# Attention of an encoder trunk: each link of the softmax chain half a slot later, and the channel-major products copied by ScalarE and split by GpSimd

## The chip, the cores and the metric

The kernel runs on one core of one Trainium2 chip. A core has five engines with instruction streams of their own, which wait for each other through semaphores: PE (TensorE: matrix products and transposes into PSUM), ACT (ScalarE), DVE (VectorE), POOL (GpSimd), and SP (SyncE, which here issues DMA transfers). Each engine works through its stream strictly in order. The metric is the time of one execution in microseconds (us).

## The reference

Two layers on a sequence of 512 frames with 1024 channels, in float32. The even layer mixes frames by causal means (the pooling mixer), the odd one by attention with 16 heads of 64 channels; each is followed by a gated feed-forward part with a short causal convolution. Only the attention matters here:

```python
q = head_rmsnorm(q.reshape(B, S, N_HEADS, HEAD_DIM), q_norm)
k = head_rmsnorm(k.reshape(B, S, N_HEADS, HEAD_DIM), k_norm)
...
s = jnp.einsum('bqhd,bkhd->bhqk', qc, kb).astype(jnp.float32) * scale + bias[None]
valid = (band_chunk + c - LEFT_CHUNKS) >= 0
s = jnp.where(valid[None, None, None, :], s, -1e30)
p = jax.nn.softmax(s, axis=-1).astype(vb.dtype)
return jnp.einsum('bhqk,bkhd->bqhd', p, vb)
...
return o @ w_o
```

A product in which float32 accuracy is wanted is made of several products of a faster matrix type: an operand is split into a rounded part ("hi") and the remainder ("lo"), and hi·hi, hi·lo and lo·hi are added up in PSUM.

## The kernel before

The 512 frames are four row tiles of 128. Before the attention loop the first of four head projections is made, and the values. The loop then runs over 64 softmax tiles in fixed order, `tiles_` (16 heads, four row tiles each); tile `t` of a head has (t+1)·128 keys. One pass `i` of the loop is called an iteration, and it has two half-slots (`place` 2i and 2i+1). The loop is written out inside a manual schedule: every engine's stream has exactly the order in which the code issues its instructions.

A tile goes through the steps of the generator `tile_of`: **scores** (two PE products into a PSUM buffer `sc`, L1046 and L1047), **bias** (one DVE instruction that adds the position bias `B` and finds the minimum, L1051), **exp** (ACT, L1054, which also sums), **recip** (DVE, L1056), **scale** (ACT, L1058), **turn** (PE transposes into a PSUM buffer `tp`, L1062), **hi** (ACT, L1066) and **lo** (DVE, L1068). After the fourth tile of a head `mix` multiplies by the values (PE, L1080, PSUM buffer `oo`); ACT copies one half (`ob`, L1087) and DVE adds (L1091), and for each pair of heads the sum is split into hi (ACT, L1292) and lo (DVE, L1296) by `split_pair`.

Between these steps stand **fillers**, PE products that the loop spreads evenly (`fill`): the three other head projections (`project_heads`, 96 products each, until iterations 3.5, 19.5 and 35.5), then 144 output products (`outputs`, PSUM `wo`, until iteration 72). The weights of a filler come by DMA, and are split by ACT (L102) and POOL (L103), from the twelfth chunk on by POOL alone (L100, L103). A projection's four results are squared on ACT (L1167), summed on DVE (L1174), brought to a reciprocal root by `norm`, `seed` and `better` (DVE L1190 to L1193 last), and scaled by four POOL instructions (L1195), each 128x512.

From each scaled projection `channel_major(p, i)` makes the channel-major operands of the pair of heads `p`: four PE transposes into a PSUM buffer `zt` (L1014), a copy to the rounded `zh` by ACT (L1018), a copy of its upper half by POOL (L1020), and lo parts by DVE, `zl` for i = 0 (L1026) or two half-height `kl` for i = 1 (L1024). Both of these read `zt` in PSUM again. Then SP moves halves between partitions by DMA (L1030). `stages` sets these steps in line, at the iterations with i % 8 in `CM` of the pair before.

`later(engine, fn, n)` puts work into a waiting list, and `extra(engine)` takes from it what has waited n half-slots, one entry at a time, or two when more than one is left. The four PSUM buffers of the tag "S" are shared by `sc`, `zt`, `tp` and `oo`: whoever wants one waits for the last reader of what was in it.

Of the kernel before, what the change touches and what calls it, by code (L numbers as in the profile page):

```python
# [17 lines left out]
F32 = mybir.dt.float32  # L18
F32R = mybir.dt.float32r
AF = mybir.ActivationFunctionType  # L20
OP = mybir.AluOpType
# [3 lines left out]
S = 512  # L25
D = 1024
# [17 lines left out]
BANKS = {"PQ": 2, "SS": 4}  # L44


LAG, LAGM = 2, 2
FE = (3.5, 19.5, 35.5)
FO = LAG + 6
CM = (2, 3)  # L50


KIND = "uuppp" + "s" * 17
# [19 lines left out]
def trunk(ctx: ExitStack, tc: tile.TileContext, xt, xT, cols, band, edge, poolw, gv, wout, wqk, wv, wo, rel, out):  # L73
    nc = tc.nc
# [14 lines left out]
    def psum(tag, name, bufs=2):  # L89
        return ps.tile([P, S], F32, name=name, tag=tag, bufs=bufs)  # L90
# [3 lines left out]
    def g_tile(name):  # L94
        return tmp.tile([P, S], F32, name=name, tag="g", bufs=6)
# [31 lines left out]
    def run(steps):  # L127
        step = None
        for step in steps:
            pass  # L130
        return step
# [231 lines left out]
    gq = consts.tile([P, 2], F32, name="gq")  # L363
# [553 lines left out]
    def attention():  # L917
# [7 lines left out]
        KL = [[big.tile([P, S], F32R, name=f"kl{b}{e}") for e in range(2)] for b in range(2)]  # L925
# [70 lines left out]
        def last_output(after):  # L996

            for d in range(KD):
                hi, lo = w[18 + d // 4]
                o = psum("PQ"[d % 2], f"wo{d}_6")  # L1000
                for p in (6, 7):
                    s = slice((d % 4 * 2 + p - 6) * P, (d % 4 * 2 + p - 5) * P)
                    yield from mm3(o, hi[:, s], lo[:, s], XS[p], XS[KD + p], p == 6, p == 7)
                nc.vector.tensor_add(X[d], o, X[d])
                after(d)
                if d == 1:
                    parts(19)

        def channel_major(p, i):

            zt = psum("S", f"zt{p}_{i}", 4)
            for t in range(TT):
                j = 4 * i + 2 * (p % 2)
                nc.tensor.transpose(zt[:, t * P:(t + 1) * P], Z[p // 2, t][:, j:j + 2, :].rearrange("p h d -> p (h d)"), ident)  # L1014
            zh, z2 = (big.tile([P, S], F32R, name=f"z{c}{p}_{i}", tag="zqk", bufs=8) for c in "h2")
            zl = None if i else g_tile(f"zl{p}_{i}")
            yield
            nc.scalar.activation(zh, zt, AF.Copy, scale=gq[:, i:i + 1])  # L1018
            yield
            nc.gpsimd.tensor_copy(z2[HD:], zh[HD:].bitcast(F32))  # L1020
            if i:
                for e in range(2):
                    hs = slice(e * HD, (e + 1) * HD)
                    nc.vector.scalar_tensor_tensor(KL[p % 2][e][hs], zt[hs], gq[hs, i:i + 1], zh[hs].bitcast(F32), op0=OP.mult, op1=OP.subtract)  # L1024
            else:
                nc.vector.scalar_tensor_tensor(zl, zt, gq[:, i:i + 1], zh.bitcast(F32), op0=OP.mult, op1=OP.subtract)  # L1026
            yield
            moves = [(z2[:HD], (z2 if i else zl)[HD:]), (zh[HD:], (zh if i else zl)[:HD])]
            for o, x in moves:
                nc.sync.dma_start(o.bitcast(F32), x if x.dtype == F32 else x.bitcast(F32))  # L1030
            QK[p, i] = (zh, z2)
# [39 lines left out]
        def mix(h):  # L1071

            p, e = divmod(h, 2)
            hs = slice(e * HD, (e + 1) * HD)
            oo = psum("S", f"oo{h}", 4)
            if p not in O2:
                O2[p] = big.tile([P, S], F32, name=f"o2_{p}", tag="o2", bufs=4)
            for c in range(2):
                for j in range(TT):
                    nc.tensor.matmul(oo[:, j * P:], V[j, h // 4][:, h % 4].rearrange("p a d -> p (a d)"),  # L1080
                                     PT[e][c][:, 4 * j:3 * j + TT].rearrange("p t q -> p (t q)"),
                                     start=j == 0 and c == 0, stop=j == TT - 1 and c == 1)
            ob = g_tile(f"ob{h}")
            other = slice(HD - e * HD, 2 * HD - e * HD)

            def copy():
                nc.scalar.activation(ob[hs], oo[other], AF.Copy)  # L1087
                later("D", add)

            def add():  # L1090
                nc.vector.tensor_add(O2[p][hs], oo[hs], ob[hs])  # L1091
                if e:
                    mixed.add(p)

            later("A", copy)

# [6 lines left out]
        for i in range(2):  # L1103
            run(channel_major(0, i))
# [11 lines left out]
        def parts(k):  # L1116

            w[k] = [wp.tile([P, 1024], F32R, name=f"hw{k}_{c}", tag=f"w{c}", bufs=2) for c in "hl"]
            split(raws[k], *w[k], None if k == 19 else nc.gpsimd, nc.gpsimd if 12 <= k < 19 else None)
# [6 lines left out]
        tiles_ = [(h, t) for h in range(H) for t in range(TT)]  # L1126
        nb = len(tiles_)
        place = 0
        waiting = {"A": [], "D": []}
        mixed, kept, moved, scaled = set(), set(), set(), set()  # L1130

        def later(engine, fn, n=1):
            waiting[engine].append((place + n, fn))

        def extra(engine, all_=False):

            n = 0
            q = waiting[engine]
            while q and q[0][0] <= place and (n == 0 or all_ or len(q) > 1 and n < 2):
                q.pop(0)[1]()  # L1140
                n += 1

# [118 lines left out]
        copied, used = set(), []  # L1261
        fillers = [(project_heads(1), 96, -3, FE[0]), (project_heads(2), 96, FE[0], FE[1]), (project_heads(3), 96, FE[1], FE[2]), (outputs(), 144, FE[2], nb + FO)]
        cur, done = 0, 0

        def fill(upto):

            nonlocal cur, done
            while cur < len(fillers):
                g, n, a, b = fillers[cur]
                due = n * (upto - a) / (b - a)  # L1270
                while done < min(due, n):
                    next(g)
                    done += 1
                if upto < b:
                    return
                run(g)
                cur, done = cur + 1, 0
# [3 lines left out]
        def step(j, name):  # L1281

            if 0 <= j < nb:
                if j not in gens:
                    assert all((tiles_[j][0] // 2, i) in QK for i in range(2))
                    gens[j] = tile_of(*tiles_[j])
                assert next(gens[j]) == name

        def split_pair(p):

            def hi():
                nc.scalar.activation(XS[p], O2[p], AF.Copy)  # L1292
                later("D", lo)

            def lo():
                nc.vector.tensor_sub(XS[KD + p], O2[p], XS[p].bitcast(F32))  # L1296
                kept.add(p)

            later("A", hi)

        def stages(p, i):

            g = channel_major(p, i)
            assert p // 2 == 0 or p // 2 in scaled
            next(g)

            def scale():
                next(g)
                later("D", low)

            def low():
                next(g)
                later("D", lambda: run(g), 2)

            later("A", scale)

        order = {mybir.EngineType.PE, mybir.EngineType.DVE, mybir.EngineType.Activation, mybir.EngineType.Pool, mybir.EngineType.SP}
        with tc.manual_schedule(engines=order):
            split_asked = 0
            fill(0)  # L1320
            for i in range(nb + LAG + LAGM):
                place = 2 * i
                step(i, "scores")
                if i % 4 == 2 and i // 4 + 1 < H:
                    biases(i // 4 + 1)
                step(i - 1, "recip")
                step(i - 3, "hi")
                step(i - 1, "scale")
                extra("A")
                extra("D")  # L1330
                step(i, "bias")
                fill(i + 0.45)
                if i % 8 in CM and i // 8 + 1 < NPAIR:
                    stages(i // 8 + 1, CM.index(i % 8))
                place = 2 * i + 1
                step(i, "exp")
                step(i - LAG, "turn")
                step(i - 3, "lo")
                extra("D")
                extra("A")  # L1340
                fill(i + 0.9)
                j2 = i - LAG - LAGM
                if 0 <= j2 < nb and j2 % TT == TT - 1:
                    mix(tiles_[j2][0])
                fill(i + 1)
                while split_asked in mixed and len(used) > 8 + split_asked // 2:
                    split_pair(split_asked)
                    split_asked += 1
            while waiting["A"] or waiting["D"] or cur < len(fillers):
                place += 1  # L1350
                extra("A", True)
                extra("D", True)
                while split_asked in mixed:
                    split_pair(split_asked)
                    split_asked += 1
                fill(min(place / 2 + 0.5, nb + FO))
        assert len(kept) == NPAIR
        return last_output
# [92 lines left out]
```

## Time and profile before

| | |
|---|---|
| time, three runs | 979.63, 979.70, 979.99 us; median 979.7 us |
| profiled execution | 980.12 us, of which the span of the trace is 978.3 us |
| granted TensorE clock | 1.00 throughout |
| scores of the first and of the last tile start | 452.37 and 606.29 us |

Times in the profile count from the start of the span. A row of the profile is a group of instructions: the source line, the engine and operation, what it writes and reads, the form, how many (x), their busy time and the mean of one, and the idle time of the engine just before them with what ended it. A PE row of 128x512 lasts 0.39 us, but such products follow each other every 0.23 us: they overlap in the pipeline. "PEld" is the loading of weights, ahead of the product.

### The profile page before, as it was taken

The page shows a single profiled execution, that of the slowest core. Times are in us where ns is not written, and L with a number is a line of the kernel's source. Part 1 is how long each engine was busy: PE and PEld are TensorE (multiplying, and loading weights), DVE is VectorE, ACT ScalarE, POOL GpSimd, SP SyncE. Part 2 cuts the span into 40 slices and gives each one's busy share as a digit, 9 for nine tenths or more (in the row PEclk, how much of TensorE's full clock was granted, in tenths as well). Part 3 has the DMA queues.
Part 4 walks back from the last instruction along what each step waited for, and adds up shares of the span by engine and source line. Part 5 has one row for each costly group of instructions (what it writes and reads, how often), then busy time and mean ns, then how long its engine had stood idle before and what let it go on. Part 6 is the DMA issues. An engine that isn't in the chain of part 4 may idle for free.

```text
span 978.3 us, 13709 instructions
## 1 busy us (share of the span) xinstructions
PE 963.7 (98%) x4982; PEld 815.6 (83%) x4982; DVE 811.7 (83%) x1461; ACT 576.5 (59%) x989; POOL 105.7 (11%) x92
## 2 busy tenths in 40 slices
PE   9999999999999999999999999999999999999998
PEld 8788988888888888888887778788988888888886
DVE  8999999999899754443777777899989999989953
ACT  7665564664555443345887888646555565556531
POOL 2300000000000013214434433100000000000000
PEclk9999999999999999999999999999999999999999
DMA  8222332332333234233343333323232342322323
GB/s 340 80 88 74 110 114 73 119 119 92 103 94 107 83 90 139 87 108 97 103 119 86 95 74 119 100 75 111 93 113 77 101 131 88 123 94 84 109 82 111
DMA packets 37427, 102.82 MB, mean 105 GB/s; under 512 B 4432, under 2 KB 7904, under 8 KB 37360
## 3 DMA queue, kind: packets, MB, share of 16 engines
q1 hardware_dynamic: 37296, 101.90, 32.8%
q8 instruction: 39, 0.64, 0.3%
q14 instruction: 28, 0.23, 0.1%
q0 software_dynamic: 32, 0.04, 0.0%
q10 hardware_dynamic: 32, 0.00, 0.0%
HBM read 95.60 MB, written 2.14 MB: 100 GB/s over the span
## 4 chain that ended last, share of the span: by engine, by line
PE 86%; DVE 6%; ACT 4%; issue 2%; DMA 1%; SPq 0%; DVEq 0%; ACTq 0%
PE st_m L610 11%; PE out L124 8%; PE out L123 8%; PE out L125 8%; PE st_m L612 6%; PE st_t L610 6%; PE gv L124 4%; PE gv L125 4%; PE gv L123 4%; PE st_t L612 3%; PE st_b L610 3%; PE qk L123 2%; PE qk L125 2%; PE qk L124 2%; PE v L124 1%
## 5 line engine op out<-in xcount | busy, mean ns | idle before, releaser
L124 PE MATMUL out<-one,ow_h 128*128 128x512 f32 x224 | 88.0, 393 | 0.0
L123 PE MATMUL out<-one,ow_h 128*128 128x512 f32 x224 | 87.9, 392 | 0.0
L125 PE MATMUL out<-one,ow_l 128*128 128x512 f32 x224 | 87.8, 392 | 0.0
L833 DVE TENSOR_TENSOR X<-out,X 128x512 f32<-128x512 f32 (+1 forms) x65 | 44.5, 685 | 48.9 <-PE out L125 48.6
L409 ACT ACTIVATE ow_h<-wo_r 128x640 fp32r<-128x640 f32 (+1 forms) x64 | 50.4, 788 | 56.2 <-PE out L124 46.3
L610 PE MATMUL st_m<-two,g_h 128*128 128x512 f32 x240 | 75.0, 394 | 0.0
L610 PE MATMUL st_m<-h,g_h 128*128 128x512 f32 x240 | 74.0, 390 | 0.0
L410 DVE TENSOR_TENSOR ow_l<-wo_r,ow_h 128x640 fp32r<-128x640 f32 (+1 forms) x64 | 57.1, 892 | 2.6 <-ACT ow_h L409 2.6
L424 DVE SCALAR_TENSOR_TENSOR c<-a,col,c 128x511 f32<-128x511 f32 (+1 forms) x76 | 57.0, 753 | 0.0
L610 PEld LDWEIGHTS st_m<-h,g_h 128*128 128x128 f32 x240 | 45.1, 188 | 10.2
L612 PEld LDWEIGHTS st_m<-two,g_l 128*128 128x128 f32 x240 | 45.1, 188 | 9.4
L610 PEld LDWEIGHTS st_m<-two,g_h 128*128 128x128 f32 x240 | 44.1, 188 | 10.0 <-ACT w L619 0.8
L103 POOL TENSOR_TENSOR hw_l<-hw_r,hw_h 128x1024 fp32r<-128x1024 f32 x19 | 45.9, 2417 | 51.9 <-ACT hw_h L102 51.3
L619 ACT ACTIVATE w<-st_m 128x512 f32<-128x512 f32 x30 | 18.0, 599 | 56.4 <-PE st_m L612 56.4
L1054 ACT ACTIVATE sb<-sb,mx 128x128 f32<-128x128 f32 (+1 forms) x64 | 35.9, 560 | 23.9 <-DVE mx L1051 23.5
L612 PE MATMUL st_m<-h,g_l 128*128 128x256 f32 x240 | 48.3, 283 | 0.0
L1051 DVE CUSTOM_DVE_ANT_0 sb<-sc,B 128x128 f32<-128x128 f32 (+1 forms) x64 | 31.0, 485 | 20.3 <-PE sc L1047 19.7
L125 PEld LDWEIGHTS out<-one,ow_l 128*128 128x128 f32 x224 | 42.3, 189 | 6.3
L612 PE MATMUL st_m<-two,g_l 128*128 128x256 f32 x240 | 47.6, 280 | 0.0
L124 PEld LDWEIGHTS out<-one,ow_h 128*128 128x128 f32 x224 | 42.4, 189 | 6.2 <-DVE one L435 0.3
L123 PEld LDWEIGHTS out<-one,ow_h 128*128 128x128 f32 x224 | 42.4, 189 | 6.1
L421 ACT ACTIVATE c<-a,col 128x512 f32<-128x512 f32 x38 | 30.7, 814 | 25.1 <-DVE a L768 23.5
(396 smaller groups left out, 2980.8 us busy)
## 6 DMA issues: line engine op xcount, KB each, us to landing
gv_r<-gv SPq DMA_DIRECT2D x86, 512.0 KB, 3.8
wo_r<-wout SPq DMA_DIRECT2D x32, 384.0 KB, 3.1
wo_r<-wout SPq DMA_DIRECT2D x32, 320.0 KB, 2.9
hw_r<-wqk SPq DMA_DIRECT2D x12, 512.0 KB, 4.0
wv_r<-wv SPq DMA_DIRECT2D x8, 512.0 KB, 3.4
hw_r<-wo SPq DMA_DIRECT2D x8, 512.0 KB, 4.5
xt<-xt SPq DMA_DIRECT2D x4, 512.0 KB, 5.2
X<-xT SPq DMA_DIRECT2D x8, 256.0 KB, 7.6
```

Of the source, the lines that this page charges most:

```text
L103: return (eng or nc.vector).tensor_sub(lo, raw, hi.bitcast(F32))
L123: yield nc.tensor.matmul(o, sh, mh, start=first, stop=False, **how)
L124: yield nc.tensor.matmul(o, sh, ml, start=False, stop=False, **how)
L125: yield nc.tensor.matmul(o, sl, mh, start=False, stop=last, **how)
L409: nc.scalar.activation(hi[:, :n], raw[:, :n], AF.Copy)
L410: return hi, lo, lambda: nc.vector.tensor_sub(lo[:, :n], raw[:, :n], hi[:, :n].bitcast(F32))
L424: nc.vector.scalar_tensor_tensor(c[:, j:], a[:, :S - j], cw[2 - j], c[:, j:], op0=OP.mult, op1=OP.add)
L610: nc.tensor.matmul(o, hi[:, c], B[i, name], start=first and i == 0, stop=False, **how)
L612: nc.tensor.matmul(o[:, 0], lo[:, c], B[i, name][:, 0], start=False, stop=i == 3, **how)
L833: nc.vector.tensor_add(X[d][:, fs], o[:, fs], X[d][:, fs])
L1051: nc.vector.tensor_tensor_reduce(out=s_, in0=sc[:, :n], in1=BT[h % 2][:, :n][:, ::-1], scale=1.0, scalar=3e38, op0=OP.add, op1=OP.min, acc ...
L1054: nc.scalar.activation(s_, s_, AF.Exp, scale=-1.0, bias=mx[:, 0:1], accum_out=mx[:, 1:2])
```

## The change

Each link of a tile's chain is issued half a slot later: exp of tile i-1 now stands in the first half of iteration i (before: exp of tile i in its second half), recip of tile i-1 in the second half, scale of tile i-2 in the second half, turn of tile i-3 (before: i-2), hi and lo of tile i-4 (before: i-3), and `mix` one iteration later. The channel-major work starts one iteration earlier (`CM` (1, 2) for (2, 3)). In it ACT first copies `zt`, scaled, to a float32 tile `zf` in SBUF, and from that makes `zh`; the lo parts are made by POOL from `zf` and `zh`, so that PSUM is read once. The DMA moves wait in a list of their own, "S". `extra` takes a second entry by another rule. The output fillers run a little slower within the loop and faster behind it.

```diff
-LAG, LAGM = 2, 2
+LAG, LAGM = 3, 2
-CM = (2, 3)
+CM = (1, 2)
...
-            nc.scalar.activation(zh, zt, AF.Copy, scale=gq[:, i:i + 1])
+            zs = g_tile(f"zf{p}_{i}")
+            nc.scalar.activation(zs, zt, AF.Copy, scale=gq[:, i:i + 1])
+            yield
+            nc.scalar.activation(zh, zs, AF.Copy)
...
-                    nc.vector.scalar_tensor_tensor(KL[p % 2][e][hs], zt[hs], gq[hs, i:i + 1], zh[hs].bitcast(F32), op0=OP.mult, op1=OP.subtract)
+                    nc.gpsimd.tensor_sub(KL[p % 2][e][hs], zs[hs], zh[hs].bitcast(F32))
...
-                nc.vector.scalar_tensor_tensor(zl, zt, gq[:, i:i + 1], zh.bitcast(F32), op0=OP.mult, op1=OP.subtract)
+                nc.gpsimd.tensor_sub(zl, zs, zh.bitcast(F32))
...
-            while q and q[0][0] <= place and (n == 0 or all_ or len(q) > 1 and n < 2):
+            while q and q[0][0] <= place and (n == 0 or all_ or n < 2 and (place < 16 or len(q) > (1 if engine == "D" else 3))):
...
+                if cur == 3:
+                    due = 104 * (upto - a) / (nb - a) if upto < nb else 104 + 5.6 * (upto - nb) if upto < nb + 5 else 132 + 3 * (upto - nb - 5)
...
-                later("D", low)
-
-            def low():
-                next(g)
-                later("D", lambda: run(g), 2)
+                later("A", high)
+
+            def high():
+                next(g)
+                next(g)
+                later("S", lambda: run(g), 5 if i else 4)
...
-                step(i - 1, "recip")
-                step(i - 3, "hi")
-                step(i - 1, "scale")
+                extra("S")
+                step(i - LAG - 1, "hi")
+                step(i - 1, "exp")
                 extra("A")
                 extra("D")
                 step(i, "bias")
...
-                step(i, "exp")
+                extra("S")
+                step(i - 2, "scale")
+                extra("A")
                 step(i - LAG, "turn")
-                step(i - 3, "lo")
+                step(i - LAG - 1, "lo")
+                step(i - 1, "recip")
                 extra("D")
-                extra("A")
```

Besides, the last split of weights (`parts(19)`) stands one output group earlier, and `split_pair` is also asked for right behind the DVE addition that completes a pair.

Where this moves instructions is seen in the streams. First ACT around the channel-major work of pair 3 (iterations 18 and 19 before, 17 and 18 after); `sb` are softmax tiles with L1054 or L1057 the exponent and L1058 or L1061 the scaling, `pt` the hi parts. Before:

```order
L1018 ACTIVATE zh_0_4814<-zt_0_4809,gq 128x512
L1066 ACTIVATE pt0h<-tp_0_4818 128x128
L1058 ACTIVATE sb_2_4803<-sb_2_4803,mx_2_4804 128x384
L1167 ACTIVATE zs_1_4833<-z_1_4821 128x512
L1054 ACTIVATE sb_3_4837,mx_3_4838<-sb_3_4837,mx_3_4838 128x512
L1159 ACTIVATE z_2_4856<-qk_2_4400 128x512
L1018 ACTIVATE zh_1_4848<-zt_1_4843,gq 128x512
```

The same place in the changed kernel:

```order
L1019 ACTIVATE zf_0_4828<-zt_0_4779,gq 128x512
L1069 ACTIVATE pt1h<-tp_3_4830 128x4x128
L1057 ACTIVATE sb_2_4814,mx_2_4815<-sb_2_4814,mx_2_4815 128x384
L1171 ACTIVATE zs_1_4846<-z_1_4812 128x512
L1061 ACTIVATE sb_1_4773<-sb_1_4773,mx_1_4774 128x256
L1019 ACTIVATE zf_1_4855<-zt_1_4820,gq 128x512
L1069 ACTIVATE pt0h<-tp_0_4857 128x128
L1057 ACTIVATE sb_3_4848,mx_3_4849<-sb_3_4848,mx_3_4849 128x512
L1021 ACTIVATE zh_0_4784<-zf_0_4828 128x512
```

Before, scaling of tile 2 came directly ahead of the exponent of tile 3; now scaling of tile 1 stands between the exponents of tiles 2 and 3, and each channel-major product has two ACT copies, the second (`zh`) some eight rows behind the first (`zf`).

Second, POOL around the scaling of the last projection (`z_2`, `z_3`, the last two of four) and the channel-major work of pair 6. Before:

```order
L1195 TENSOR_TENSOR z_2_5364<-z_2_5364,qk_y 128x512
L1195 TENSOR_TENSOR z_3_5407<-z_3_5407,qk_y 128x512
L1020 CAST z_0_5570<-zh_0_5569 64x512
L100 CAST hw_h<-hw_r 128x1024
L103 TENSOR_TENSOR hw_l<-hw_r,hw_h 128x1024
L1020 CAST z_1_5602<-zh_1_5601 64x512
```

After:

```order
L1199 TENSOR_TENSOR z_2_5400<-z_2_5400,qk_y 128x512
L1199 TENSOR_TENSOR z_3_5391<-z_3_5391,qk_y 128x512
L1023 CAST z_0_5555<-zh_0_5554 64x512
L1029 TENSOR_TENSOR zl_0_5556<-zf_0_5558,zh_0_5554 128x512
L1023 CAST z_1_5594<-zh_1_5593 64x512
L1027 TENSOR_TENSOR kl_3629<-zf_1_5596,zh_1_5593 64x512
L1027 TENSOR_TENSOR kl_3630<-zf_1_5596,zh_1_5593 64x512
```

Three subtractions for each pair have come into POOL's stream, between the scaling and the splitting of weights.

Third, PE at the transposes of pair 6, which read the four scaled tiles. Before, they stood in iteration 42, behind the scores of tile 2 of head 10:

```order
L1046 MATMUL sc_2_5550<-zh_1_5356,zh_0_5322 128x384
L1047 MATMUL sc_2_5550<-kl_3631,zh_0_5322 128x384
L125 MATMUL wo_0_5545<-two_96,hw_l 128x512
L123 MATMUL wo_0_5545<-two_96,hw_h 128x512
L1014 MATMUL zt_0_5564<-ident,z_0_5278 128x128
L1014 MATMUL zt_0_5564<-ident,z_1_5329 128x128
L1014 MATMUL zt_0_5564<-ident,z_2_5364 128x128
L1014 MATMUL zt_0_5564<-ident,z_3_5407 128x128
```

After, they stand in iteration 41, behind the scores of tile 1:

```order
L1049 MATMUL sc_1_5539<-zh_1_5341,zh_0_5300 128x256
L1050 MATMUL sc_1_5539<-kl_3631,zh_0_5300 128x256
L123 MATMUL wo_0_5397<-two_97,hw_h 128x512
L1014 MATMUL zt_0_5549<-ident,z_0_5287 128x128
L1014 MATMUL zt_0_5549<-ident,z_1_5328 128x128
L1014 MATMUL zt_0_5549<-ident,z_2_5400 128x128
L1014 MATMUL zt_0_5549<-ident,z_3_5391 128x128
L1065 MATMUL tp_2_5560<-ident,sb_2_5460 128x128 x3
```

They have moved up by one iteration, and the transposes of a softmax tile (`tp`) follow them at once.

More of the change, by code (lines that the diff above doesn't have):

```diff
@@ L1004, in last_output @@
                 nc.vector.tensor_add(X[d], o, X[d])
+                if d == 0:
+                    parts(19)
                 after(d)
-                if d == 1:
-                    parts(19)
         def channel_major(p, i):
@@ L1093, in add @@
                     mixed.add(p)
+                    split_pairs()
             later("A", copy)
@@ L1128, in attention @@
         place = 0
-        waiting = {"A": [], "D": []}
+        waiting = {"A": [], "D": [], "S": []}
         mixed, kept, moved, scaled = set(), set(), set(), set()
@@ L1299, in split_pair, with split_pairs @@
             later("A", hi)
+        split_asked = 0
+        def split_pairs():
+            nonlocal split_asked
+            while split_asked in mixed and len(used) > 8 + split_asked // 2:
+                split_pair(split_asked)
+                split_asked += 1
         def stages(p, i):
@@ L1318, in attention @@
         with tc.manual_schedule(engines=order):
-            split_asked = 0
             fill(0)
@@ L1345, in attention @@
                 fill(i + 1)
-                while split_asked in mixed and len(used) > 8 + split_asked // 2:
-                    split_pair(split_asked)
-                    split_asked += 1
+                split_pairs()
             while waiting["A"] or waiting["D"] or cur < len(fillers):
                 place += 1
+                assert not waiting["S"]
                 extra("A", True)
                 extra("D", True)
-                while split_asked in mixed:
-                    split_pair(split_asked)
-                    split_asked += 1
                 fill(min(place / 2 + 0.5, nb + FO))
```

## The prediction

> **What bounds the kernel now.** I begin with the engines' shares on the page, and the chain that ended last.
>
> ```profile
> PE 963.7 (98%) x4982; PEld 815.6 (83%) x4982; DVE 811.7 (83%) x1461; ACT 576.5 (59%) x989; POOL 105.7 (11%) x92
> PE 86%; DVE 6%; ACT 4%; issue 2%; DMA 1%; SPq 0%; DVEq 0%; ACTq 0%
> ```
>
> PE is busy 98% of the span, and the change neither adds nor removes a PE product. It can win only time in which PE waits, within the loop that it touches. So the second view is busy time by stretches. I cut the loop at the starts of the scores of every eighth tile, so that each row is one pair of heads (the last one is what follows the loop).
>
> ```profile
> core 0: us, PE busy (x) PEld busy (x) DVE busy (x) ACT busy (x) POOL busy (x), PEclk, DMA share, GB/s
> 452.37:476.88 24.51, 24.21 (x124) 20.26 (x123) 13.58 (x44) 18.21 (x43) 8.92 (x6) 1.00 0.33 89
> 476.88:496.26 19.38, 19.38 (x109) 16.49 (x109) 12.01 (x37) 16.05 (x39) 9.54 (x8) 1.00 0.46 135
> 496.26:516.81 20.55, 19.69 (x110) 16.42 (x109) 16.36 (x48) 17.40 (x43) 6.62 (x5) 1.00 0.35 97
> 516.81:539.20 22.39, 20.28 (x108) 16.39 (x109) 16.32 (x42) 18.71 (x45) 11.29 (x10) 1.00 0.37 93
> 539.20:558.61 19.41, 18.02 (x101) 14.59 (x100) 16.28 (x49) 16.58 (x43) 6.86 (x6) 1.00 0.38 107
> 558.61:577.11 18.50, 16.68 (x93) 13.23 (x94) 14.16 (x44) 15.66 (x40) 9.95 (x10) 1.00 0.33 83
> 577.11:594.40 17.29, 16.04 (x93) 13.10 (x91) 14.07 (x41) 14.07 (x36) 6.60 (x5) 1.00 0.32 92
> 594.40:609.29 14.89, 14.89 (x87) 12.61 (x87) 12.18 (x39) 12.95 (x36) 3.45 (x2) 1.00 0.41 123
> 609.29:630.00 20.71, 20.19 (x93) 16.17 (x93) 17.18 (x27) 14.49 (x23) 3.44 (x2) 1.00 0.39 118
> ```
>
> PE's idle time is length less busy: 0.30, 0, 0.86, 2.11, 1.39, 1.82, 1.25, 0 and 0.52 us, together **8.25 us**. A stop costs more than that, because a product's row lasts longer than the distance to the next one:
>
> ```profile
> 525.72 0.40 PE L123 MATMUL qk<-hw_h,two 128*128 128x512 f32 x1
> 525.96 0.39 PE L124 MATMUL qk<-hw_l,two 128*128 128x512 f32 x1
> ```
>
> Rows of 0.40 us start 0.24 us apart, so the first 0.16 us of a stop still count as busy. The second to fourth stretches hold the same products (109, 110 and 108 records), and the second has no stop: against its 19.38 us the next two are 1.17 and 3.01 us longer, for 0.86 and 2.11 us of idle rows. That is a factor of 4.18/2.97 = 1.41, and all stops cost about 8.25 × 1.41 = **11.6 us**. More than this the change cannot win. The view of waits, PE alone from 445 to 640 us, says on what:
>
> ```profile
> PE tp L1062 <- DVE kl L1024: 3.5, 5, 0.8
> PE sc L1046 <- DVE mx L1051: 2.6, 3, 1.3
> PE tp L1062 <- DVE zl L1026: 0.7, 2, 0.5
> PE sc L1046 <- DMA zh<-zh: 0.3, 1, 0.3
> PE wo L125 <- DVE hw_l L103: 0.2, 1, 0.2
> ```
>
> The first and third are one thing: transposes of a softmax tile wait for a PSUM buffer that the lo parts of the channel-major work still read, 4.2 us of rows, so 5.9 us. Scores that wait for the bias instruction of an earlier tile: 2.6, so 3.7 us. The rest is 8.25 - 6.8 = 1.45, so 2.0 us.
>
> **What is removed.** The lo parts no longer read PSUM:
>
> ```profile
> L1024 DVE SCALAR_TENSOR_TENSOR kl<-zt,gq,zh 64x512 fp32r<-64x512 f32 x14 | 10.5, 749 | 3.5 <-ACT zh L1018 3.4
> L1026 DVE SCALAR_TENSOR_TENSOR zl<-zt,gq,zh 128x512 f32<-128x512 f32 x7 | 5.3, 751 | 3.1 <-ACT zh L1018 2.9
> L1018 ACT ACTIVATE zh<-zt,gq 128x512 fp32r<-128x512 f32 x14 | 9.4, 673 | 0.3 <-PE zt L1014 0.3
> ```
>
> Before, a `zt` buffer came free after 0.67 us of ACT, an idle gap ahead of the first (3.4 us before `kl` and 2.9 before `zl`, in all), and one or two DVE rows of 0.75 us; now it is free after the one ACT copy (of the same form as L1018, so 0.67 us). The 5.9 us go whole; what is late next is that ACT copy, priced below. DVE is relieved of 14 × 0.75 + 7 × 0.75 = 15.8 us. It was busy 115 us of the 157 us of the first eight stretches and is then near 99. With this, and with a whole iteration between the exponent and its reciprocal, the bias instructions come earlier. They were late where DVE had work in front of them; the worst such place is a score 1.34 us late, behind a DVE instruction that ran long:
>
> ```profile
> 525.15 0.50 PE L1046 MATMUL sc<-zh,zh 128*128 128x512 f32 x1 [1.34 <-DVE mx L1051]
> 522.58 1.98 DVE L1296 TENSOR_TENSOR two<-o,two 128x512 fp32r<-128x512 f32 x1
> 521.63 2.38 POOL L103 TENSOR_TENSOR hw_l<-hw_r,hw_h 128x1024 fp32r<-128x1024 f32 x1 [1.36 <-ACT hw_h L102]
> L1296 DVE TENSOR_TENSOR two<-o,two 128x512 fp32r<-128x512 f32 x8 | 8.2, 1029 | 0.4 <-ACT two L1292 0.2
> ```
>
> Eight of these have a mean of 1.03 us, and one took 1.98 us while POOL worked. Such meetings stay, and POOL will be busier; so I count 2.7 of the 3.7 us as gone, with bounds of 1.0 and 3.7. The Trainium skill, "SBUF — State Buffer", section "Who interferes with whom", says that a DVE instruction with two SBUF inputs contends with a GpSimd instruction that reads SBUF, and that the later one blocks; the 1.98 us agree with that. By that page alone each of the eight could meet one of POOL's new subtractions, and the term would fall to its lower end, the sum to 976.0 us. Of the remaining 2.0 us I count 0.9 as gone (0 to 1.5): the wait for `hw_l` goes with the earlier `parts(19)`, the DMA wait may stay. Removed: 5.9 + 2.7 + 0.9 = **9.5 us**.
>
> The view of waits has larger rows than these, and they are no gain:
>
> ```profile
> ACT sb L1054 <- DVE mx L1051: 23.5, 33, 4.2
> DVE mx L1056 <- ACT sb L1054: 14.3, 34, 0.8
> ```
>
> ACT and DVE wait for each other in the chain of a tile, 38 us. The change takes most of that away, since now exp follows its bias by a half-slot and recip its exp by another. But neither engine is the bound, and where PE runs without a stop (the second stretch) they wait as well.
>
> **What is added: a later scaling for earlier transposes.** The first transposes of pairs 4 and 6 read a projection that POOL scales only after `better`. They move up one iteration (41 for 42, 25 for 26).
>
> ```profile
> L1195 POOL TENSOR_TENSOR z<-z,qk_y 128x512 f32<-128x512 f32 x12 | 12.1, 1044 | 10.5 <-DVE qk_y L1193 7.6 <-DVE mx L1056 2.8
> 516.22 4.05 POOL L1195 TENSOR_TENSOR z<-z,qk_y 128x512 f32<-128x512 f32 x4 [2.93 <-DVE qk_y L1193]
> 558.03 4.05 POOL L1195 TENSOR_TENSOR z<-z,qk_y 128x512 f32<-128x512 f32 x4 [4.72 <-DVE qk_y L1193]
> 562.85 0.63 PE L1014 MATMUL zt<-ident,z 128*128 128x128 f32 x4
> 560.45 0.40 PE L124 MATMUL wo<-two,hw_h 128*128 128x512 f32 x1
> 519.11 0.40 PE L123 MATMUL qk<-hw_h,two 128*128 128x512 f32 x1
> 557.87 0.69 DVE L1051 CUSTOM_DVE_ANT_0 sb<-sc,B 128x512 f32<-128x512 f32 x1
> ```
>
> For pair 6 the scaling ended at 558.03 + 4.05 = 562.08, and the transposes came at 562.85. In the new place they stand behind one output product, the one at 560.45, so they would be wanted at 560.7, and the last of the four 0.3 us later, at 561.0 (the four have a row of 0.63 us): 1.1 us before the last scaled tile. `better` now stands behind the bias of tile 39 (the 0.69 us at 557.87) instead of ahead of it, but that bias began only 0.7 us ahead of the scores of tile 40 (558.61), in iterations of some 2.4 us; DVE ran late there and will be less late. I let the start lie between 1.1 us earlier and 1.0 later, which gives a wait of 0 to 2.1 us, and take 1.4. For pair 4 the scaling ended at 520.27, and the transposes are wanted behind the three products that begin at 519.11, at 519.8, the last at 520.1: 0 to 1.2, I take 0.6. Together **2.0 us** (0 to 3.3).
>
> **ACT.** It gets 14 more copies of 128x512 from SBUF within the loop:
>
> ```profile
> L1167 ACT ACTIVATE zs<-z 128x512 f32<-128x512 f32 x12 | 7.5, 623 | 0.0
> ```
>
> Two in each stretch but the last, 1.2 us. PE's needs without stops are 19.4 us in the fourth stretch, 19.41 - 1.39 × 1.41 = 17.4 in the fifth, 15.9 in the sixth and 15.5 in the seventh. ACT then needs 19.9, 17.8, 16.9 and 15.3: 0.5, 0.4 and 1.0 us more than PE in three of them. Its rows overlap by about 0.1 us back to back, so this shortage of 1.9 us is an upper end; I take **1.2 us** (0 to 1.9).
>
> **A buffer within one iteration.** At the first transposes of each pair after the first, `zt` has taken one more buffer, and the following `tp` needs the one that the bias of the same iteration frees. PE's cover is one to three products of 0.23 us and four short transposes. If DVE is held by one reciprocal or lo part, it is late by a few tenths: seven times 0.13, **0.9 us** (0 to 1.8).
>
> **POOL.** The 21 subtractions have the form of L1195, 1.04 us (bounds for a half-height one: 0.61 us by the row below, 1.04 us), 21.8 us in the loop.
>
> ```profile
> L1020 POOL CAST z<-zh 64x512 fp32r<-64x512 f32 x14 | 8.5, 611 | 31.3 <-ACT zh L1018 22.3 <-issue 8.0 <-POOL hw_l L103 0.8
> L103 POOL TENSOR_TENSOR hw_l<-hw_r,hw_h 128x1024 fp32r<-128x1024 f32 x16 | 38.7, 2420 | 31.2 <-ACT hw_h L102 30.6
> z<-z SPq DMA_DIRECT2D x8, 128.0 KB, 2.2
> ```
>
> POOL's 63 us of the first eight stretches become 85 of about 150, so its own work is covered. An operand is needed by the scores two iterations (4 us) after its lo part; the move takes 2.2 us to land, so I cost this at nothing, and up to 1.5 us if POOL's queue is late. The Trainium skill, "GPSIMD Engine Reference", section "4.1 Engine selection", advises against elementwise work with two inputs on this engine, as about 2 times slower than VectorE. The rows say 1.04 against 0.75 us, 1.4 times. With a factor of 2 the subtractions would take 21 × 1.5 = 31.5 us and POOL 95 of 150 us, which would still be covered, but would bring the third rival below closer.
>
> **The sum.** 9.5 - 2.0 - 1.2 - 0.9 = 5.4 us. Against the profiled execution, 980.12 us, that is 974.7; the median of the runs lies 0.4 us below it, so **974.3 us**.
>
> **Rivals.**
> (a) *All waits added are hidden.* After one stop each later engine has caught up, so the three added terms overlap: only the 2.1 us of old waits stay, a gain of 9.5 us, **970.2 us**. For it speaks that DVE loses 14% of its work; against it that POOL's scaling is a chain that nothing shortens.
> (b) *ACT takes the place.* The second copy and the shortage fall into the same stretches as the scaling; ACT's lag of up to 1.9 us is then met again by every following wait of scores and transposes, 4 us more than I count. The gain is 1.4 us: **978.3 us**. ACT at 18.7 of 22.4 us in the fourth stretch speaks for it.
> (c) *Slower: POOL's queue in order.* Ahead of the last scaling POOL now has two subtractions for pair 5 and the splitting of a weight chunk by itself, 1.04 + 2.42 us. If these begin just before `better` ends, scaling starts 3.5 us later, pair 4 loses 2.1 us by its two subtractions in the same way, and the next weight chunk comes late for the output products, 2 to 3 us: 8 us against a gain of 5.4, **982.3 us**. It decides once scaling starts over about 3 us behind `better` at both places. Against it: POOL waited 4.72 and 2.93 us ahead of them.
> (d) *The chain was no cause.* The freed buffers only move PE's wait on to the bias or to the turning of the next tile, since PE meets the same chain a moment later: no change, **979.7 us**. Against it stands the second stretch, where the same chain has no stop.
>
> **How the numbers follow.** Chances: forecast 0.52 (972 to 976.5), (a) 0.20, (b) 0.14, (c) 0.08, (d) 0.06. A measurement of this kernel tells about 0.2%, 2 us, from no change, so faster means below 977.7: the forecast, (a) and a little of (b), 0.75. Slower is (c), 0.08; the rest, 0.17, is the same. For 8 in 10 the range leaves out (c), half of (d) and the far end of (a): 969.5 to 979.7 us.
>
> **What would show it.** In the changed profile the waits of `tp` on `kl` and `zl` are gone, and DVE's time in the first eight stretches is near 99 us. `zt` waits for POOL at two places, about 1.4 and 0.6 us. PE's idle in the nine stretches is near 4.4 us (6.2 us by 1.41) instead of 8.25. Were waits on POOL over 4 us, (c) is right; many waits of `tp` or `sc` on ACT mean (b). Idle time as before with other names at its side would make the prediction wrong, and so would a stop outside the loop.

## The result: slower, and the profile after

| | before | after |
|---|---|---|
| median | 979.74 us (6 runs, 979.63 to 982.19) | 983.59 us (6 runs, 982.22 to 985.79) |
| ratio | | 1.0036, 95% interval 1.0020 to 1.0052 |
| profiled execution, span | 980.12, 978.3 us | 982.51, 980.7 us |
| mean granted clock | 1.0 | 0.994 to 0.998, in every run |

The change makes the kernel 0.36% slower. The forecast was 974.3 us, range 969.5 to 979.7. The first view is again busy time by stretches of the profiled execution, cut at the starts of the scores of every eighth tile; the columns are as before (PE, PEld, DVE, ACT, POOL, then clock and DMA).

```profile
452.30:474.96 22.66, 22.66 (x114) 18.82 (x113) 11.38 (x36) 16.43 (x39) 12.50 (x9) 1.00 0.37 115
474.96:494.28 19.32, 19.32 (x109) 16.50 (x108) 9.84 (x38) 17.07 (x43) 13.66 (x11) 1.00 0.39 108
494.28:516.31 22.03, 19.75 (x110) 16.37 (x108) 14.16 (x45) 20.29 (x51) 9.91 (x7) 1.00 0.26 75
516.31:537.08 20.77, 19.84 (x108) 16.59 (x109) 12.46 (x40) 17.50 (x42) 15.39 (x12) 1.00 0.42 121
537.08:556.74 19.66, 17.43 (x99) 14.46 (x98) 12.71 (x40) 17.57 (x46) 10.13 (x9) 1.00 0.29 79
556.74:575.33 18.59, 17.11 (x90) 14.28 (x91) 12.62 (x43) 15.09 (x40) 14.15 (x12) 0.91 0.37 84
575.33:593.52 18.19, 15.82 (x90) 12.66 (x89) 13.91 (x43) 16.27 (x44) 10.77 (x10) 1.00 0.28 76
593.52:609.79 16.27, 16.10 (x90) 13.67 (x91) 11.00 (x39) 12.27 (x34) 5.02 (x3) 1.00 0.46 141
609.79:630.00 20.21, 20.21 (x99) 16.78 (x98) 15.93 (x26) 12.13 (x20) 3.44 (x2) 1.00 0.36 115
```

Length less busy time gives PE idle of 0, 0, 2.28, 0.93, 2.23, 1.48, 2.37, 0.17 and 0 us: 9.5 us, where before it was 8.25. DVE has lost what it was to lose (98 us in the first eight stretches, from 115), POOL has 92 for 63. And in one stretch the clock is 0.91. The view of waits shows PE's idle time under quite different names, and the same view of SP's queue (DMA issues) what the last of them comes from.

```profile
PE sc L1049 <- DMA zh<-zh: 3.1, 2, 1.7
PE sc L1049 <- DVE qk_t L1194: 2.3, 1, 2.3
PE wo L124 <- DVE two L1302: 1.5, 1, 1.5
PE zt L1014 <- POOL z L1199: 0.9, 2, 0.7
PE wo L123 <- DVE z L1161: 0.9, 1, 0.9
PE tp L1065 <- DVE mx L1054: 0.5, 1, 0.5
...
SPq L1033 <- POOL kl L1027: 14.8, 8, 2.2
```

The many waits of `tp` on `kl` and `zl` are gone, and those of scores on the bias but for 0.2 us. In their place stand a few long ones. Three of them are the first scores of heads 6, 10 and 14, at the heads of the odd pairs 3, 5 and 7. One is put down to `qk_t` on DVE, which the scores do not read; the timelines of POOL, SP and PE there (start, length, engine, what) show that a DMA lands just ahead of it, as for the other two:

```profile
508.05 2.41 POOL L103 TENSOR_TENSOR hw_l<-hw_r,hw_h 128x1024 fp32r<-128x1024 f32 x1
510.52 0.61 POOL L1023 CAST z<-zh 64x512 fp32r<-64x512 f32 x1
511.21 2.71 POOL L1027 TENSOR_TENSOR kl<-zf,zh 64x512 fp32r<-64x512 f32 x2
...
511.16 0.46 SPq L1033 DMA_DIRECT2D z<-z  x1
513.95 0.46 SPq L1033 DMA_DIRECT2D zh<-zh  x1
...
516.31 0.36 PE L1049 MATMUL sc<-zh,zh 128*128 128x256 f32 x1 [2.28 <-DVE qk_t L1194]
```

The second move, `zh<-zh`, writes the lower half of `zh` over its upper half, and POOL's second subtraction still has to read that upper half. POOL ends at 513.92, SP issues the move at 513.95, such a move lands 2.2 us later (the median), and the scores begin at 516.31; PE's last product before them ended at 514.03. Before the change DVE read that half straight after ACT had written it, and the move was issued 8.5 us ahead of the same scores (516.81):

```profile
506.68 1.51 DVE L1024 SCALAR_TENSOR_TENSOR kl<-zt,gq,zh 64x512 fp32r<-64x512 f32 x2 [0.90 <-ACT zh L1018]
508.26 0.46 SPq L1030 DMA_DIRECT2D zh<-zh  x1
```

The other two are put down to the move itself (1.3 and 1.7 us).

### The profile page after: what moved, and what is told of

It reads as the page before. It is cut to its first block, busy times and chain, and to the rows that moved or that the text cites. A ratio compares the mean times of both kernels' runs of the same rounds, so it can differ in the third digit from the quotient of the medians.

```text
span 980.7 us, 13735 instructions
## 1 busy us (share of the span) xinstructions
PE 964.4 (98%) x4982; PEld 817.4 (83%) x4982; DVE 793.9 (81%) x1437; ACT 580.1 (59%) x1005; POOL 137.4 (14%) x116
## 4 chain that ended last, share of the span: by engine, by line
PE 89%; DVE 6%; ACT 3%; issue 1%; DMA 1%; POOL 0%; DVEq 0%; SPq 0%; ACTq 0%; POOLq 0%
PE st_m L610 11%; PE out L124 8%; PE out L125 8%; PE out L123 8%; PE st_m L612 6%; PE st_t L610 6%; PE gv L124 3%; PE gv L125 3%; PE gv L123 3%; PE st_t L612 3%; PE st_b L610 3%; PE qk L125 3%; PE qk L123 3%; PE qk L124 3%; PE oo L1083 2%; PE v L124 1%
## 5 line engine op out<-in xcount | busy, mean ns | idle before, releaser
L1054 DVE CUSTOM_DVE_ANT_0 sb<-sc,B 128x128 f32<-128x128 f32 (+1 forms) x64 | 31.2, 487 | 59.8 <-PE sc L1050 57.1
L148 POOL TENSOR_TENSOR n_acc<-n_acc,n_sq 128x512 f32<-128x512 f32 x7 | 9.6, 1368 | 328.1 <-ACT n_sq L146 328.1
```

The source lines that it names most:

```text
L1054: nc.vector.tensor_tensor_reduce(out=s_, in0=sc[:, :n], in1=BT[h % 2][:, :n][:, ::-1], scale=1.0, scalar=3e38, op0=OP.add, op1=OP.min, acc ...
```

## The experiments

Each kernel was timed in several rounds beside the kernel before on the same chip. The edits are shown against the changed kernel unless said otherwise. The interval of the changed kernel itself is 1.6 us to either side, so smaller differences to it show little by themselves.

| kernel | median, us | ratio to before | 95% interval |
|---|---|---|---|
| e1_swap | 982.48 | 1.0024 | 1.0013 to 1.0036 |
| e2_order_alone | 976.54 | 0.9965 | 0.9953 to 0.9977 |
| e3_split_alone | 991.52 | 1.0118 | 1.0104 to 1.0133 |
| e4_odd_early | 981.65 | 1.0009 | 1.0001 to 1.0018 |
| e5_even_late | 973.62 | 0.9932 | 0.9918 to 0.9945 |
| e6_copies_dve | 987.53 | 1.0073 | 1.0060 to 1.0085 |
| e7_zf_dve | 980.48 | 0.9999 | 0.9991 to 1.0008 |
| e8_copy_first | 972.47 | 0.9920 | 0.9906 to 0.9933 |
| e9_no_overwrite | 982.47 | 1.0022 | 1.0013 to 1.0031 |
| e10_all_early | 978.87 | 0.9987 | 0.9978 to 0.9995 |
| e11_best | 974.25 | 0.9939 | 0.9927 to 0.9952 |
| e12_two_turns | 978.78 | 0.9984 | 0.9975 to 0.9993 |
| e13_no_overwrite_zf_dve | 977.39 | 0.9974 | 0.9965 to 0.9982 |
| e14_no_overwrite_two_turns | 976.86 | 0.9968 | 0.9955 to 0.9980 |
| e15_split_best | 977.86 | 0.9974 | 0.9965 to 0.9983 |

### The two halves of the change

**e2_order_alone** keeps the new order and puts the old channel-major work back, with the moves where the changed kernel has them:

```diff
-            zs = g_tile(f"zf{p}_{i}")
-            nc.scalar.activation(zs, zt, AF.Copy, scale=gq[:, i:i + 1])
-            yield
-            nc.scalar.activation(zh, zs, AF.Copy)
+            nc.scalar.activation(zh, zt, AF.Copy, scale=gq[:, i:i + 1])
...
-                    nc.gpsimd.tensor_sub(KL[p % 2][e][hs], zs[hs], zh[hs].bitcast(F32))
+                    nc.vector.scalar_tensor_tensor(KL[p % 2][e][hs], zt[hs], gq[hs, i:i + 1], zh[hs].bitcast(F32), op0=OP.mult, op1=OP.subtract)
```

> The new order with the old channel-major work: ScalarE makes zh straight from PSUM, VectorE the lo parts from PSUM. Theory A: the waits of the first scores on the moves go (6 us), but waits of tp on kl and zl come back in part; 975 to 979 us. Rival B (ScalarE's load): also faster, 976 to 980 us, but with ScalarE's busy time 8 us lower in the loop being what changed. Rival C (the order itself makes the loss): 982 us or more.

**e3_split_alone** is the reverse: the old order, with `channel_major` as the change has it.

> The old order with the new channel-major work (copy to zf, zh from zf by ScalarE, subtractions by POOL). Theory A: the work begins one iteration later than in the changed kernel, so the moves land later still, at every pair: waits of scores on moves above 6 us, 984 to 990 us, while waits of tp on lo parts are gone. Rival C (order): no slower than before, 976 to 980 us.

Measured: 976.5 us, and 991.5 us, which is above what was expected of e3. So the order gains 0.35%, and the new channel-major work costs 7.1 us on the new order (983.6 less 976.5) and about 12 us on the old. The waits of PE in e2 are these, with the three largest of e3 behind them:

```profile
PE zt L1014 <- POOL z L1196: 3.2, 5, 0.7
PE wo L123 <- ACT z L1160: 1.2, 1, 1.2
PE qk L123 <- ACT z L1160: 0.3, 1, 0.3
PE sc L1046 <- ACT pt0h L1066: 0.2, 1, 0.2
...
PE sc L1049 <- DVE mx L1054: 5.9, 5, 1.8
PE tp L1065 <- DVE mx L1054: 2.7, 3, 1.7
PE sc L1049 <- DMA zh<-zh: 2.6, 1, 2.6
```

Two things are to be seen. There is no wait of `tp` on `kl` or `zl`, though in e2 VectorE still reads `zt` in PSUM: the order is enough to take these 4.2 us of rows away. The copy to SBUF is enough as well, since e3 has none of them either; but there PE waits 8.6 us for the bias, which in e2 it does not. And in e2 the transposes of pairs 4 and 6 wait 3.2 us for the scaling of their projection.

### One suspect at a time

**e1_swap**, `for e in (1, 0):`, lets POOL read the upper half first.

> The two half-height subtractions of a pair change places, so that the one that reads the upper half of zh comes first. Theory A (the second DMA move of a pair overwrites that upper half, so it stands in SP's queue until POOL has read it, and the first scores of heads 6, 10 and 14 wait for the landing): the move is issued about 1.3 us earlier in each pair, the three waits of scores on the move shrink by up to 1.3 us each, in all 3 to 4 us: 979 to 980.5 us. Rival B (ScalarE's second copy makes zh late, POOL's order does not matter): 983 to 984 us, waits as they were. Rival C (the wait for the scaling of the projection and the lower clock behind it): 983 to 984 us.

**e9_no_overwrite** lets the second subtraction read POOL's own copy of the upper half, so that the move waits for no subtraction:

```diff
-                    nc.gpsimd.tensor_sub(KL[p % 2][e][hs], zs[hs], zh[hs].bitcast(F32))
+                    nc.gpsimd.tensor_sub(KL[p % 2][e][hs], zs[hs], (z2 if e else zh)[hs].bitcast(F32))
```

> The changed kernel, but the subtraction for the upper half reads POOL's own copy of that half instead of zh, so that the second move, which overwrites it, need not wait for the subtractions, only for the copy. Nothing else is moved. Theory A (the moves wait for POOL to have read what they overwrite): the move is issued some 2.6 us earlier in each pair, waits of first scores on a move fall below 0.5 us in all; as with the exchanged subtractions much of it comes back as waits of the transposes of pairs 4 and 6 on the scaling (4 to 5 us by starts): 980 to 982 us. Rival (the moves are late for another reason, SP's queue or the landing): waits and time as in the changed kernel, 983 to 984 us.

**e4_odd_early** starts the odd pairs one iteration earlier, `cm = CM if i // 8 % 2 else (0, 1)`.

> The changed kernel with the channel-major work of the odd pairs (3, 5, 7) one iteration earlier. Theory A: the three waits on moves (2.3, 1.3 and 1.7 us by rows, 6 us by starts) vanish, and with them the low clock behind the longest idle time: 976 to 978.5 us. Rival B (ScalarE's load sets the pace): 982 to 984 us. Rival C (scaling): 982 to 984 us.

Measured: 982.5, 982.5 and 981.7 us. e1 and e4 lie between what their theories gave, and e9 just above its first. In e9 the mechanism is as said: the row of SP's waits on `kl` (14.8 us in the changed kernel) is gone, and no score waits for a move. But the time is hardly less than in the changed kernel (the intervals overlap). Its waits of PE show where it went:

```profile
PE zt L1014 <- POOL z L1199: 3.1, 5, 1.1
PE sc L1049 <- DVE o L1094: 1.8, 2, 1.2
PE wo L124 <- DVE two L1302: 1.5, 1, 1.5
PE wo L123 <- DVE z L1161: 0.9, 1, 0.9
PE sc L1049 <- DVE mx L1054: 0.6, 1, 0.6
PE tp L1065 <- DVE mx L1054: 0.5, 1, 0.5
```

The wait for the scaling rises from 0.9 to 3.1 us as soon as PE comes earlier, and the first scores of heads 6 and 10 wait for a PSUM buffer that the sum of an earlier head (`o`) frees. At head 6 that sum stands in VectorE's stream behind a small instruction of the projection, which took 1.16 us while POOL subtracted:

```profile
511.85 0.59 ACT L1090 ACTIVATE ob<-oo 64x512 f32<-64x512 f32 x1
512.73 1.16 DVE L1184 TENSOR_SCALAR qk_a<-qk_a 128x32 f32<-128x32 f32 x1
513.92 0.69 DVE L1094 TENSOR_TENSOR o<-oo,ob 64x512 f32<-64x512 f32 x1
```

ACT's copy `ob`, which the sum also needs, had ended 1.5 us before. What looked like one cause is a stack of delays, each hidden behind the next. e4 says the same: three waits gone, 2 us won.

### ACT: load or list

**e7_zf_dve** lets VectorE make `zf` (`nc.vector.tensor_scalar(zs, zt, gq[:, i:i + 1], None, op0=OP.mult)`, and `later("D", scale)`), so that ACT has one copy for each product as before.

> The changed kernel, but VectorE makes the scaled copy zf, so that ScalarE has one copy for each product, as before the change; POOL keeps the subtractions. Theory A: the moves still wait for POOL, 981 to 984 us. Rival B (ScalarE): 976 to 979 us.

**e6_copies_dve** keeps ACT's two copies and lets VectorE make the lo parts from `zf` and `zh` in SBUF.

> The changed kernel, but VectorE makes the lo parts, from zf and zh in SBUF; ScalarE keeps its two copies. Tells ScalarE's second copy from POOL's subtractions, between the changed kernel (983.6 us) and the new order with the old work (976.5 us). Theory A (POOL's subtractions hold the moves): 976 to 979 us, no wait of the first scores on a move over 0.5 us. Rival B (ScalarE's second copy): 981 to 984 us, first scores late as before.

e7 took 980.5 us, between the two theories: ACT's part is about 3 us. e6 took 987.5, and neither theory had that: with POOL out, it should have been near 977. Its rows say why:

```profile
L1027 DVE TENSOR_TENSOR kl<-zf,zh 64x512 fp32r<-64x512 f32 x14 | 16.1, 1149 | 0.2
L1023 POOL CAST z<-zh 64x512 fp32r<-64x512 f32 x14 | 11.9, 849 | 35.2 <-ACT zh L1021 21.6 <-issue 11.5 <-PE tp L1065 1.3
```

A subtraction of two SBUF operands on VectorE takes 1.15 us in the mean, where the one with a PSUM operand took 0.75, but between 0.66 and 2.49 us, and the longest ran beside POOL's splitting of weights. POOL's copy takes 0.85 instead of 0.61. So the two engines hold each other up, and behind the subtractions in VectorE's stream the bias comes late (PE's scores wait 6.3 us for it). So e6 does not tell ACT from POOL; it brings in a third cost.

**e12_two_turns** leaves all work on the engines where the change has put it and takes back only the rule of the waiting lists (but for the first eight iterations, `place < 16`):

```diff
-            while q and q[0][0] <= place and (n == 0 or all_ or n < 2 and (place < 16 or len(q) > (1 if engine == "D" else 3))):
+            while q and q[0][0] <= place and (n == 0 or all_ or n < 2 and (place < 16 or len(q) > 1)):
```

> The changed kernel with the old rule of the waiting lists: ScalarE takes two entries in a half-slot whenever more than one is left (in the changed kernel only from four on). Theory Q (each product now has one more entry in ScalarE's list, one is taken per half-slot, and zh and the copy ob come out of it an iteration later; so the subtractions and moves start late): zh of the odd pairs comes about 2 us earlier, waits of first scores on moves mostly gone, 978 to 981 us. Rival (ScalarE's load, not its list): ScalarE is as busy as before, 983 to 984 us.

Measured: 978.8 us, 4.8 less, with ACT as busy as before (130.2 us between the first and the last scores, 130.3 in the changed kernel). So what it won back was not ACT's load, but the turn in the list. With the change each channel-major product has two entries in ACT's list instead of one; one entry is taken per half-slot unless more than three are left behind it, and `zh` and `ob` wait their turn. The timeline of POOL in e12 shows the subtractions of pair 3 over 4 us earlier than in the changed kernel (511.21 there), and the weight chunk behind them instead of ahead:

```profile
506.29 0.61 POOL L1023 CAST z<-zh 64x512 fp32r<-64x512 f32 x1 [1.96 <-issue]
506.98 2.64 POOL L1027 TENSOR_TENSOR kl<-zf,zh 64x512 fp32r<-64x512 f32 x2
509.70 2.40 POOL L103 TENSOR_TENSOR hw_l<-hw_r,hw_h 128x1024 fp32r<-128x1024 f32 x1
```

One score still waits 1.7 us for a move (head 14). And the old rule serves more than the channel-major work: a projection's copies and squares stand in the same list, and no transpose waits for the scaling any more.

### Two together

**e13_no_overwrite_zf_dve** is e7 with the edit of e9, **e14_no_overwrite_two_turns** is e12 with the edit of e9.

> Two of the suspected costs taken away together: the move need not wait for the subtractions, and VectorE makes zf, so that ScalarE has one copy for each product. If the two are costs in series, each hidden behind the other: 976 to 978.5 us, below either alone (982.5 and 980.5). If they are the same wait: 980 to 981 us.

> The changed kernel with the old rule of the lists and with the move that need not wait for the subtractions; both copies on ScalarE, the subtractions on POOL. If list and overwriting are the two delays: 977 to 979.5 us, and what is left are the waits for the scaling. If ScalarE's load or POOL's collisions with VectorE carry the loss: 981 us or more.

Measured: 977.4 and 976.9 us. The overwriting, worth 1 us by itself, is worth 3.1 and 1.9 us once ACT's delay is gone. e14 keeps both ACT copies and all of POOL's subtractions, and is level with e2 (976.5), the new order with the old work: the list and the overwriting together return 6.7 of the 7.1 us. e13, which keeps the new rule and takes one of the two ACT copies away instead, returns 6.2. What is left in e14 is not what was expected:

```profile
PE tp L1065 <- DVE mx L1054: 2.9, 3, 1.3
PE zt L1014 <- POOL z L1199: 0.2, 1, 0.2
```

Where e2 waits 3.2 us for the scaling, e14 waits 0.2 for it and 2.9 for the bias. The two are level with different waits, and e2 with the old rule of the lists was not run. So how much of what the rule returns was lost by the new work, and how much it would win without that work, is open.

### Toward a faster version

**e5_even_late** is e2 with the even pairs one iteration later (`cm = (2, 3) if i // 8 % 2 else CM`), **e8_copy_first** is e5 with the copy of a finished projection at the head of its list (`waiting[...].insert(0, ...)`), **e11_best** is e8 with the third projection one iteration earlier, **e10_all_early** is e4 with earlier projections and that copy first.

> The new order with the old channel-major work (976.5 us), and the work of the even pairs (2, 4, 6) one iteration later, where it stood before the change. Theory D (what is left are the transposes of pairs 4 and 6 that wait for the scaling of their projection, 4.3 us by starts): 972 to 974 us. Rival (the waits go over to the moves of these pairs, which are then later too): 975.5 to 977 us.

> The kernel before in this list, and the copy of a finished projection out of PSUM goes to the head of its waiting list, so that the first output products need not wait for the buffer. If that wait (1.5 us by starts in the new order with the old work) is on the path: 1 to 1.5 us below the kernel before in this list. If the chain of the scaling or of the softmax ends last there: the same within 0.5 us.

> The best version so far (new order, old channel-major work, even pairs one iteration later, the copy first) with the third head projection done one iteration earlier. If the remaining 0.9 us wait for the scaling and the stops around it are the projection's chain: 971 to 972 us. If they are the softmax chain's: 972.3 to 973 us.

> The changed kernel with ScalarE's two copies and POOL's subtractions kept, and each of the late things given more room: odd pairs one iteration earlier, the second and third head projections done one iteration earlier (so that the scaling is), and the copy of a finished projection at the head of its list. Theory L (what the new work costs is delay, not load: ScalarE and POOL have the time): 974 to 977 us. Rival (load: ScalarE's 130 us and POOL's 90 us in the loop hold PE wherever the work stands): 979 to 982 us.

Measured: 973.6, 972.5, 974.3 and 978.9 us. e5 and e8 do what their theories said: without the earlier transposes of pairs 4 and 6 the wait for the scaling is 0.7 us (in e8). e11 misses: an earlier projection makes other waits. e10 fell between its two cases. e8 is the fastest, 0.8% below the kernel before; its waits of PE are down to

```profile
PE oo L1080 <- ACT pt0h L1066: 0.7, 1, 0.7
PE zt L1014 <- POOL z L1196: 0.7, 1, 0.7
PE tp L1062 <- ACT sb L1058: 0.3, 1, 0.3
PE oo L1080 <- DVE mx L1051: 0.2, 1, 0.2
```

**e15_split_best** has everything found, with the change's split kept.

> Everything found, with the change's own split kept (two ScalarE copies, subtractions by POOL): old rule of the lists, no overwriting, even pairs one iteration later, the copy of a finished projection first. Against the same kernel with the old channel-major work (972.5 us). If the split frees PSUM to a gain once its delays are gone: below 972 us. If it only moves work, and ScalarE's second copy and the meetings of POOL and VectorE still cost: 973 to 976 us. If even pairs then come late as the odd ones did: above 977 us.

Measured: 977.9 us, 5.4 more than e8. Its waits of PE are `tp` on the bias (3.0 us) and again a score on a move (1.7 us, head 12: pair 6, now later). So no run showed a gain from the split: with its delays removed in the changed order it is level (e14 with e2), and in the better order it costs. Both comparisons also differ in the rule of the lists, which is the old one in e14 and e15 and the new one in e2 and e8. In e15's trace the clock is 0.89 and 0.94 in the two stretches of 10 us from 550 us on, 1.7 us together; how the rest of the 5.4 us divides between the late move, the bias and the rule was not tried.

## Why the prediction was wrong

**Where the time is.** That PE's waits in the loop decide the time was right, but not that they are all: the clock adds to them (below).

**Removed, 9.5 us.** The waits that made it up are gone, but for 0.2 us of rows on the bias. The reason given for the largest part was only half of it. The 5.9 us were put down to lo parts that no longer read PSUM, and e3 bears out that this is enough; but e2 loses the same waits with the lo parts in PSUM. On top of the order the split had nothing left to remove.

**The step that failed: "I cost this at nothing, and up to 1.5 us if POOL's queue is late".** That was the price of the subtractions and moves, on the ground that an operand is needed two iterations (4 us) after its lo part. At head 6 the second lo part ended at 513.92, and PE was free for the scores at 514.03. The chain from `zt` to the moves had become longer at three places that were not followed: a second entry in ACT's list, of which one is taken per half-slot; the subtractions, 1.29 us each and not 1.04, in POOL's stream behind a weight chunk of 2.41 us (at pairs 3 and 7); and a move that overwrites what the second of them reads. Taking the first and the third away returns 6.2 of 7.1 us with the new rule of the lists (e13). The new rule of `extra` was in the diff, and no term of the sum spoke of it; taking it back returns 4.8 us (e12), and 6.7 with the overwriting (e14).

**The scaling, 2.0 us (0 to 3.3).** The mechanism is right. In the changed kernel PE lost only 0.9 us of rows there, since longer stops just ahead hid the rest. In the new order without them it is 3.2 us of rows, 4.5 by the factor of 1.41; taking 2.5 of the 3.2 away won 2.9 us (e5). So it was mis-sized, at its upper bound or beyond.

**ACT, 1.2 us.** Argued from busy time. At the same busy time e12 is 4.8 us faster: the turn in the list mattered more. What the busy time costs by itself was not separated.

**The buffer within one iteration, 0.9 us.** 0.5 us of rows, 0.7 by the factor: about right.

**The rivals.** Slower was given 0.08, with POOL's queue in order as the cause, but at the scaling, more than 3 us behind `better`. The scaling began 0.1 us behind it (558.89 after a DVE row that ended at 558.81). It was the same queue at another place. Nothing was foreseen of the clock, which adds the rest:

```profile
556.00:559.40 3.40, 1.26 (x6) 0.83 (x6) 3.20 (x11) 2.83 (x9) 2.52 (x2) 0.96 0.24 46
559.40:563.40 4.00, 3.93 (x16) 3.52 (x17) 0.76 (x6) 1.29 (x4) 3.91 (x4) 0.61 0.63 162
```

PE is busy 1.26 of 3.40 us, between a late move and the split of a pair on DVE that comes late; in the following 4 us it is granted 0.61 of its clock. That is 4 × 0.39 = 1.6 us, which counts as busy time. With the 1.2 us more of idle rows (1.7 by the factor) it makes 2.8 to 3.3 us, by estimate, where the two profiled executions are 2.4 us apart. The medians are 3.85 us apart: the profiled execution was the second fastest of the changed kernel's six, and what the slower ones lost besides stands in no trace.

## What to carry to other kernels

When work goes over to an idle engine, follow its whole chain to the instruction that needs the result, with each list and queue that it stands in, and look for what later overwrites its inputs: an in-place move waits for the slowest reader. Idle time of the new engine says nothing of that delay. And where undoing one suspect returns little, try two together before acquitting it: delays in series hide each other.

## What the runs showed of the hardware

In the changed kernel the granted clock fell behind a stretch in which PE mostly waited, though no single stop in it was long: the two stops above are 1.3 and 1.5 us by rows. The traces of e3, e6, e9 and e14 also hold stretches of 10 us in the loop at 0.83, so 1.7 us each; the trace of e2 holds none. The Trainium skill, "TensorE: Matmul & The Clock Gate", section "Part 1: The HAM clock gate (the "warmup" mystery)", says that the clock halves after an idle window of some 3.4 us, and that the window is free-running. The 0.61 agrees with a half clock for most of those 4 us, and the free-running window would fit that the same kernel sometimes meets it and sometimes not: e2 ran 976.3 us at a mean clock of 1.0, and 977.4 and 977.6 at 0.997 and 0.998. But here PE was not idle through such a window: it was busy 1.26 of 3.40 us.

POOL's subtraction took 1.29 us where its product of the same size (with a small second operand that is read repeatedly) took 1.04 before and 1.15 in the mean after. Small VectorE instructions met it: one of 128x32, 0.18 us before, took 1.16 us at 512.80, during the subtractions. The second row gives the shortest, the median and the longest of POOL's half-height subtractions in ns.

```profile
512.80 1.16 DVE L1184 TENSOR_SCALAR qk_a<-qk_a 128x32 f32<-128x32 f32 x1
L1027 POOL TENSOR_TENSOR kl<-zf,zh x14: 1279/1289/1352, 465.6 to 589.9; 64x512 fp32r<-64x512 f32 x14
```

The seven of full height took 1.28 to 1.30 us, no more than those of half the height. With so little spread their length hardly comes from meetings. Why a subtraction takes longer than a product was not tried.
